# An encoder kernel on one core: layer 0 projects in float32 without splits, u is rearranged by copies, RoPE in six operations, a new order of the work

## The chip, the cores and the metric

The kernel runs on one core of one Trainium2 chip. The metric is the device time of one execution in microseconds. A core has TensorE (PE, matrix products into PSUM), VectorE (DVE), ScalarE (ACT), GpSimd (POOL), and SyncE (SP), which in this kernel only issues DMAs.

## The reference

Two pre-norm layers work on 256 tokens of width 1024 in float32. Each layer has a token mixer and a mixture of experts:

```
xn = rmsnorm(x, ln1_g);  proj = xn @ w_in
qa, ka, va, u, cq, ckv, kr = split(proj)        # 384 128 128 256 192 128 32 columns
o_attn = windowed_gqa(qa, ka, va, sink)         # 6 heads, 2 kv heads, window 128, ALiBi
o_ssm  = s5_bidirectional(u, ...)               # 16 groups x 64 complex states, two directions, GLU
o_mla  = mla(cq, ckv, kr, ...)                  # 6 heads of 64 + 32 rotary, low-rank q and kv
x = x + concat(rmsnorm each of the three) @ w_out
x = x + hier_moe(rmsnorm(x, ln2_g), ...)        # 4 groups x 8 experts, top group, top 2 of it
```

Each expert has a gate, an up (1024 x 256) and a down matrix (256 x 1024). After the two layers comes a last rmsnorm. RoPE turns the 32 rotary columns of q (six heads) and of the one shared key: (x1 cos - x2 sin, x1 sin + x2 cos).

## The kernel before, in words

**Buffers.** All weights stream through a ring of 25 SBUF buffers of 128 x 2048 float32 (1 MB each). SP issues their DMAs in one fixed order: the mixer's weights (u, nat, qk, mla, gr, o), then for each block of experts the gate and up halves and the down matrices, then layer 1. The mixer's temporaries take buffers of the same ring. `make_plan` counts from the written order how many temporaries each step needs, and `room` lets a weight be fetched only if the steps up to its use still have their buffers. When no buffer is free, the stream stands still.

**Order.** `SEQ` is a string for each layer: the mixer's steps in the order in which they are emitted, each with letters that choose the engine of its optional operations (V VectorE, S ScalarE, G GpSimd). The framework then orders each engine's instructions around that. Steps of the mixer: x (transposed input), u, n0 n1 (columns in token order: va, cq, ckv, kr), q0 to q3 (columns transposed: q and k), uc (u by place), t0 to t4, td, i, w, c (tables of the state space layer), s0 s1 (its products with the inputs), S0 S1 (its scans, one direction each), so and gl (its output and GLU), a/A/V (scores, weights, values of the windowed attention), la lq lk lv l0 to l2 lr m/M/W (the same of the latent attention), G (norms of the groups), O (output projection by group, token half, column half), R r e h k (router).

**Splits.** For the letters in `SPLIT` of a layer a float32 product is made of three passes in float32r: `parts` makes a rounded high half on ScalarE and the low half on VectorE or GpSimd (line 672), `halved` does it for the input of layer 0 (line 717), and `mm` (line 682) issues high x high, high x low, low x high. Layer 0 splits n and q, layer 1 u, n and q, and the output projection is split in both; `finish` writes its left side as a high and a low half (line 854). Without a split `mm` issues one float32 product.

**u by place.** `u_chunks` picks every fourth token of u and sets the four picks on top of each other, 32 channels each, with 32 products with slices of the identity (line 748), and one copy out of PSUM.

**RoPE.** `latent_q` makes six operations for each token half, all on the engine that one letter picks (lines 955 to 960).

**Experts.** `moe` gathers each expert's tokens by products with one-hot matrices, four or two experts beside each other in TensorE's columns (line 1441 gate and up, line 1457 down), and adds the results back to x. A block's buffers come free as its products end.

Of the kernel before, what the change touches and what calls it, by code (L numbers as in the profile page):

```python
# [22 lines left out]
T = 256  # L23
# [5 lines left out]
SEQ = ("x:VSGGVSVG t1 x0:V x1:G t2:GVGSSV pn0:GGGG t3 pn1:VGGG x3:V sq x2:V u b0 n0 rb:SVV pq0:GVVV n1:SVVS "  # L29
# [10 lines left out]
SPLIT = ("nq", "unq")  # L40
# [10 lines left out]
        "gl": ("ub", "qkv", "hT", "hTl"), "R": KEEP, "r0": KEEP, "r1": KEEP, "e0": KEEP, "e1": KEEP, "h0": (), "h1": (), "k0": (), "k1": (),  # L51
# [111 lines left out]
def hybrid_encoder_kernel(ctx, tc, I, out, dbg=None):  # L163
# [402 lines left out]
    def uses(l, w):  # L566

        hs = ["hT", "hTl"]
# [6 lines left out]
        if w in USES:  # L575
            u = list(USES[w])
# [7 lines left out]
        elif w[0] == "p":  # L584
            u = wp(w[1], w[1:])
        elif w[0] == "P":
            u = [f"o{w[1]}h", f"o{w[1]}l"]
        elif w[0] in "aA":
            u = ["PB" if w[1] == "2" else "PA"] + (["qkv", "bs"] if w[0] == "a" else ["pt"])
        elif w[0] == "m":  # L590
            u = ["qT", "kT", "PB" if w[1] in "45" else "PM"]
        elif w[0] == "M":
            u = ["PB" if w[1] == "2" else "PM", "pt"]
        elif w[0] in "VW":
            u = ["pt", "ub", "qkv" if w[0] == "V" else "cTvm"] + hs
        elif w[0] == "O":
            u = [f"o{int(w[1]) + i}{p}" for i in range(2) for p in "hl"] + hs
        else:
            u = []
        return u  # L600

    def eats(l, w):
# [9 lines left out]
        if w[0] == "P":  # L612
            return [(l, "o", int(w[1]))]
        return [(l, "gr")] if w in ("gl", "e0", "e1") else []

    def mixer(l):
# [10 lines left out]
        def hs():  # L627
            return [sub(n, 0, (8, T)).bitcast(F32R) for n in ("hT", "hTl")]
# [56 lines left out]
        with tc.tile_pool(name=f"mx{l}", bufs=1, reuse_waits="tile") as mp:  # L685
# [7 lines left out]
            def transposed():  # L693

                xT = xs("u")
                for k in range(8):
# [10 lines left out]
                    pk = p[:, 256 * (k % 2):256 * (k % 2) + 256]  # L707
                    S.activation(xT[0][:, k, :], pk, AF.Copy, scale=g)
# [35 lines left out]
            def u_chunks():  # L744
                u4p = ps("u4p")
                for j in range(4):
                    for i in range(8):
                        PE.matmul(u4p[32 * j:32 * j + 32, 64 * i:64 * i + 64], ident[:, 32 * (i % 4):32 * (i % 4) + 32],
                                  uT()[:, i // 4, :].rearrange("p (q j) -> p j q", j=4)[:, j, :],
                                  start=True, stop=True, tile_position=(0, 32 * j))  # L750
                copy(u4().rearrange("p i q -> p (i q)"), u4p)
# [98 lines left out]
            def finish(c, g, k, vg, src):  # L850
# [3 lines left out]
                V.scalar_tensor_tensor(hT[1][:, k, :], src, gc, hT[0][:, k, :].bitcast(F32), op0=OP.mult, op1=OP.subtract)  # L854
# [84 lines left out]
            def latent_q():  # L939
                mw, q, ra4 = page(l, "mla"), qn(), sub("qn", 1344, (4, 7, 16))  # L940
                G.memset(q[:, :, 6, 0:64], 0.0)
                for tt in range(2):
# [7 lines left out]
                    G.tensor_copy(q[:, tt, 6, 64:96], nat()[:, tt, 320:352])  # L950
                for tt in range(2):
                    x1, x2 = q[:, tt, :, 64:80], q[:, tt, :, 80:96]
                    cb, sb = cos[:, tt].to_broadcast([128, 7, 16]), sin[:, tt].to_broadcast([128, 7, 16])
                    e = pick("VG")
                    e.tensor_tensor(ra4[:, 0], x1, cb, OP.mult)
                    e.tensor_tensor(ra4[:, 1], x2, sb, OP.mult)
                    e.tensor_tensor(ra4[:, 2], x1, sb, OP.mult)
                    e.tensor_tensor(ra4[:, 3], x2, cb, OP.mult)
                    e.tensor_tensor(x1, ra4[:, 0], ra4[:, 1], OP.subtract)
                    e.tensor_tensor(x2, ra4[:, 2], ra4[:, 3], OP.add)  # L960
# [94 lines left out]
            def out_proj(g, tt, hf):  # L1055
                k0, n = ((0, 3), (3, 2), (5, 3))[g]
                p, hT = ps("op"), hs()
                for k in range(k0, k0 + n):
                    mm(p, [t[:, k, 128 * tt:128 * tt + 128] for t in hT],
                       [w[:, k % 2, 512 * hf:512 * hf + 512] for w in win[f"o{k // 2}"]], k == k0, k == k0 + n - 1)  # L1060
# [46 lines left out]
    class Router:  # L1107


        def __init__(self, l):  # L1110
# [16 lines left out]
            self.xk = x.rearrange("p t (d k) -> p t k d", k=8)  # L1127

# [4 lines left out]
        def tokens(self, tt):  # L1133
            S.activation(self.junk, x[:, tt, :], AF.Square, accum_out=self.ssq[:, tt:tt + 1])
# [561 lines left out]
```

## Time and profile before

| what | value |
|---|---|
| median of 3 runs | 772.03 us (771.19 to 775.95) |
| the profiled execution: time, span | 773.82 us, 772.0 us |
| PE busy | 654.1 us, 85% of the span |
| DVE, ACT, POOL busy | 384.6, 256.6, 162.5 us |
| moved by DMA | 232.93 MB, mean 302 GB/s |

The span runs from the first to the last instruction. Busy time of an engine is the time in which at least one of its instructions ran; matrix products are pipelined, so a busy PE is not PE at its peak. The granted clock is the mean clock that TensorE was given in a stretch, as a share of full speed. Layer 0's mixer takes the first 174 us or so, layer 1's about 403 to 525 us; the expert layers follow them.

### The profile page before, as it was taken

What the parts mean: (1) busy time and instruction counts of PE and PEld (TensorE: products, weight loads), DVE (VectorE), ACT (ScalarE), POOL (GpSimd) and SP (SyncE); (2) the same over time, 40 slices, a digit from 0 to 9 for tenths busy, and PEclk for the clock granted to TensorE, in tenths of its full rate; (3) what the DMA queues carried; (4) which work ended last, traced back from release to release, by engine and by line L of the source; (5) the groups of instructions that cost most, each with busy time, mean ns of one, the idle gap of its engine ahead of it and who ended that gap; (6) DMA issues with size and microseconds to landing.
All of it is one profiled execution on the core that took longest, in us unless ns stands there. A gap on an engine that the chain in (4) does not pass through costs nothing. (4 is left out here: it accounts for less than half of the span.)

```text
span 772.0 us, 12384 instructions
## 1 busy us (share of the span) xinstructions
PE 654.1 (85%) x4546; PEld 406.7 (53%) x4546; DVE 384.6 (50%) x872; ACT 256.6 (33%) x574; POOL 162.5 (21%) x180
## 2 busy tenths in 40 slices
PE   7599498998979778669889989998989988859994
PEld 6388386774425425135538967785545334324342
DVE  3978975643233413842436868863343232422324
ACT  2563477432201212442325268614212111011113
POOL 2654634300000001332004254530000000000001
PEclk9799797999989989878999999998999999979998
DMA  8910017489799979999999153599599999997991
GB/s 304 420 68 1 0 46 284 134 315 411 300 410 407 412 246 414 414 410 413 406 405 402 58 175 110 198 356 391 197 416 408 402 409 414 415 378 287 410 366 59
DMA packets 57209, 232.93 MB, mean 302 GB/s; under 512 B 6048, under 2 KB 8480, under 8 KB 48160
## 3 DMA queue, kind: packets, MB, share of 16 engines
q1 hardware_dynamic: 57120, 231.75, 77.5%
q8 instruction: 55, 0.90, 0.5%
q14 instruction: 34, 0.28, 0.1%
HBM read 233.82 MB, written 1.05 MB: 304 GB/s over the span
## 5 line engine op out<-in xcount | busy, mean ns | idle before, releaser
L1441 PE MATMUL gu<-pg,xe 128*32 128x512 f32 (+1 forms) x1024 | 150.1, 624 | 10.0 <-DMA pg<-in_w_up_dram 8.1
L1457 PE MATMUL yp<-pg,scr 128*32 128x512 f32 (+2 forms) x560 | 79.0, 633 | 26.8 <-DVEq L1588 12.7
L1441 PEld LDWEIGHTS gu<-pg,xe 128*32 128x32 f32 (+1 forms) x1024 | 45.1, 118 | 100.7 <-issue 94.3
L1227 POOL TENSOR_TENSOR pgt<-oh,gate 128x256 f32<-128x256 f32 (+1 forms) x13 | 10.2, 783 | 314.0 <-PE slp L373 304.7
L1235 PE MATMUL gp<-oh,xn 128*128 128x128 f32 (+1 forms) x416 | 71.1, 325 | 3.7 <-DVE oh L1220 1.6
L1235 PEld LDWEIGHTS gp<-oh,xn 128*128 128x128 f32 x416 | 61.4, 197 | 17.2 <-issue 12.3
L1457 PEld LDWEIGHTS yp<-pg,scr 128*32 128x32 f32 (+1 forms) x560 | 22.6, 120 | 73.0 <-issue 56.9
L1360 DVE TENSOR_TENSOR y<-yp,y 128x512 fp32r<-128x512 f32 (+1 forms) x39 | 26.2, 676 | 68.3 <-ACT y L1359 68.3
L1252 DVE TENSOR_TENSOR x<-cp,x 128x512 f32<-128x512 f32 x76 | 48.8, 683 | 20.2 <-PE cp L1251 20.2
L1347 DVE SCALAR_TENSOR_TENSOR scr<-gu,gs,scr 128x256 f32<-128x256 f32 x19 | 9.1, 481 | 87.1 <-ACT scr L1346 83.1
L1359 ACT CAST y<-yp 128x512 fp32r<-128x512 f32 (+1 forms) x39 | 22.3, 575 | 88.6 <-PE yp L1457 87.1
L356 ACT ACTIVATE xe<-gp,vec 128x128 f32<-128x128 f32 (+1 forms) x52 | 21.3, 409 | 73.1 <-PE gp L1235 73.1
L360 DVE TENSOR_SCALAR xe<-gp,vec 128x128 f32<-128x128 f32 (+1 forms) x52 | 20.8, 400 | 48.4 <-PE gp L1235 48.3
L1346 ACT ACTIVATE scr<-gu 128x256 f32<-128x256 f32 x19 | 7.3, 384 | 98.3 <-PEq L1558 50.7
L1250 PE MATMUL cp<-y,sm 128*128 128x512 f32 x76 | 33.5, 450 | 0.3 <-PEq L1558 0.2
L1251 PE MATMUL cp<-y,sm 128*128 128x512 f32 x76 | 30.0, 403 | 1.5 <-DVE y L1360 1.5
L1062 DVE SCALAR_TENSOR_TENSOR x<-op,rg,x 128x512 f32<-128x512 f32 x24 | 17.9, 747 | 17.4 <-PE op L682 14.2
L1340 ACT ACTIVATE scr<-slp 128x256 f32<-128x256 f32 x20 | 7.7, 387 | 46.4 <-SPq L1423 27.6
L1250 PEld LDWEIGHTS cp<-y,sm 128*128 128x128 f32 x76 | 14.3, 189 | 10.4 <-issue 8.2
L373 PE MATMUL slp<-cst,pgt 128*128 128x128 f32 x36 | 8.3, 314 | 12.1 <-DVE oh L1220 6.1
L373 PE MATMUL hp<-cst,scr 128*128 128x128 f32 x40 | 9.2, 312 | 10.9 <-DVE scr L1347 9.8
L549 PE MATMUL t4p<-ca,tabs 128*32 128x32 f32 (+3 forms) x512 | 16.3, 250 | 2.0 <-issue 2.0
(460 smaller groups left out, 1353.1 us busy)
## 6 DMA issues: line engine op xcount, KB each, us to landing
pg<-in_w_gate_dram SPq DMA_DIRECT2D x128, 512.0 KB, 10.2
pg<-in_w_up_dram SPq DMA_DIRECT2D x128, 512.0 KB, 10.2
pg<-in_w_down_dram SPq DMA_DIRECT2D x56, 1024.0 KB, 12.1
pg<-in_w_o_dram SPq DMA_DIRECT2D x8, 1024.0 KB, 17.9
pg<-in_w_down_dram SPq DMA_DIRECT2D x12, 512.0 KB, 10.4
pg<-in_w_qk_dram SPq DMA_DIRECT2D x4, 1024.0 KB, 16.3
pg<-in_w_nat_dram SPq DMA_DIRECT2D x4, 960.0 KB, 14.2
wgu<-in_w_gate_dram SPq DMA_DIRECT2D x4, 512.0 KB
```

Of the source, the lines that this page charges most:

```text
L356: S.copy(dst, src) if scale is None else S.activation(dst, src, AF.Copy, scale=scale)
L360: e.tensor_scalar(dst, src, scale, None, op0=OP.mult)
L373: PE.transpose(dst, src, ident[:src.shape[0], :src.shape[0]])
L1062: V.scalar_tensor_tensor(xh, p, rg[:, g, tt:tt + 1], xh, op0=OP.mult, op1=OP.add)
L1235: PE.matmul(p[:, :w], xn[:, tt, k, :], P[:, tt].rearrange("p e c -> p (e c)"), start=(tt == 0), stop=(tt == 1))
L1250: PE.matmul(p, Sm[:, 128 * tt:128 * tt + 128], yh[:, c], start=True, stop=False)
L1251: PE.matmul(p, Sm[:, 128 * tt:128 * tt + 128], yl[:, c], start=False, stop=True)
L1252: V.tensor_tensor(x[:, tt, c], p, x[:, tt, c], OP.add)
L1359: S.copy(yh[:, c], yp)
L1360: V.tensor_tensor(yl[:, c], yp, yh[:, c].bitcast(F32), OP.subtract)
L1441: PE.matmul(gu[m * s:m * s + m, :].rearrange("p (a f) -> p a f", a=2), xs(k, s), page(l, "gu", e, hf)[:, :, k % 4, :], start=(k == 0), sto ...
L1457: PE.matmul(yp[m * s:m * s + m, :], hT[:, j, m * s:m * s + m], page(l, "dn", e)[:, j, c], start=(j == 0), stop=(j == 1), tile_position=(0, ...
```

## The change

Layer 0 no longer splits anything: n, q and the output projection are float32 products on the weights as they arrived, and the input and the left side of the output projection exist once. So the steps pn, pq, P and x0 to x3 leave layer 0's order, `O` eats the weight buffers itself, and the split buffers are not taken. u is rearranged in both layers by 16 copies of 32 partitions (the letters behind uc alternate VectorE and ScalarE). RoPE is four products over both halves and all heads and two sums over both token halves, on VectorE. Layer 0 has a new order and new letters, most of which move work from GpSimd to VectorE or ScalarE. The router takes its two buffers at its first use (`pages`, called by `tokens`) and not at R.

```diff
--- before.py
+++ after.py
@@ -26,18 +26,17 @@
 ORDER = (((24, 2), (0, 4), (4, 4), (26, 2), (8, 4), (12, 4), (16, 4), (20, 4), (28, 4)),
          ((16, 2), (0, 4), (18, 2), (4, 4), (8, 4), (12, 4), (20, 4), (24, 4), (28, 4)))
 UNIT_PREP, UNIT_AT, TAB_AT = (3, 4), (3, 5), 4
-SEQ = ("x:VSGGVSVG t1 x0:V x1:G t2:GVGSSV pn0:GGGG t3 pn1:VGGG x3:V sq x2:V u b0 n0 rb:SVV pq0:GVVV n1:SVVS "
-       "ue i0:VVVSSVVVSS q1 w0:SSSV uc:S q0 b1 i1:GGVVSGGVSS w1:SSSV la:VVVSVSS pq1:VVVG s0 td:G q3 "
-       "S0:VGVVGG s1 a0 S1:GGGGGG b2 lq:SSSSVV a1 lk:SSSSSS q2 A0:VVSSVS l1:S lr c0:GGVVVSSVGVSS l0:V a2 "
-       "c1:VVVSVVVGVV R V0:V l2:V A1:VVVVVV m1 lv:SS t4 P1:GVGG V1:SG m3 m5 A2:GGSGGS P0:VVVV m2 m0 V2:VG so "
-       "M0:SSSSSV m4 G0 gl:VSG M1:SSSSSS W0:S P2:GVGG O000 G1 O010 W1:VV M2:GSVVGS P3:VVVV O110 W2:SV O100 "
-       "O001 G2 O201 O101 O200 O211 r0:VS O011 e0 O210 O111 h0 r1:VV e1 h1 k0 k1:V",
-       "b0 pu:GGGV x sq u rb:VVV ue pn0:GVVV b1 n0 uc:V pq0:GVGV s0 pn1:VVVG S0:VVVVVV q1 s1 pq1:GGVG "
-       "n1:SVSS S1:GGGVVG q0 q3 q2 la:SSSSSSV a0 lk:SVSSVV b2 a1 a2 lq:SSSSVV P0:GGGG so A0:SGSSSS R lv:VV "
-       "l0:S A1:GGVGGV l1:V lr V0:V l2:S A2:VSVVGV m2 V1:SG V2:SG m1 m5 m3 P1:VGGV m4 m0 G0 O000 gl:VVV O011 "
-       "M0:VVSGVS M1:VSSVGV W0:S M2:SVSVVV W1:VV P2:GGGG W2:VG G1 O111 O001 P3:GVGV O010 G2 O201 O101 O200 "
-       "O100 O110 O211 O210 r0:VV r1:VS e0 e1 h1 h0 k0 k1:V")
-SPLIT = ("nq", "unq")
+SEQ = ("x:VSSSSVVV t1 t2:GVVSVV u t3 sq b0 i0:VVVSSVVVSS n0 rb:SVV n1:SSVV ue uc:VVVSVSVSVSVSVSVS q1 w0:SSSV "
+       "i1:VVVVVVVVSV q0 w1:VSSS la:SVSSVSV s0 td:V q3 b1 S0:VVVVVV s1 a0 b2 c0:GGVVVSSVVVSS lq:SSSS lk:SSSSSS a1 q2 "
+       "A0:SVVSVS l1:S lr l2:V lv:SS l0:S S1:VVVVVV m2 c1:VVVSVVVVVV m1 V0:V a2 R A1:SSSVSS t4 A2:VVSSVS m3 m5 m0 m4 "
+       "V1:SV V2:SV so M0:VSVSVV G0 gl:VVV M1:SVSSSS W0:V M2:VSVVVS O000 G1 O010 O110 W2:SV O101 W1:SV O100 O001 O011 "
+       "G2 O201 O200 O211 r0:VV O210 e0 h0 O111 r1:VV e1 h1 k1:V k0",
+       "b0 pu:GGGV x sq u rb:VVV ue pn0:GVVV b1 n0 uc:VSVSVSVSVSVSVSVS pq0:GVGV s0 pn1:VVVG S0:VVVVVV q1 s1 pq1:GGVG "
+       "n1:SVSS S1:GGGVVG q0 q3 q2 la:SSSSSSV a0 lk:SVSSVV b2 a1 a2 lq:SSSS P0:GGGG so A0:SGSSSS R lv:VV l0:S "
+       "A1:GGVGGV l1:V lr V0:V l2:S A2:VSVVGV m2 V1:SG V2:SG m1 m5 m3 P1:VGGV m4 m0 G0 O000 gl:VVV O011 M0:VVSGVS "
+       "M1:VSSVGV W0:S M2:SVSVVV W1:VV P2:GGGG W2:VG G1 O111 O001 P3:GVGV O010 G2 O201 O101 O200 O100 O110 O211 O210 "
+       "r0:VV r1:VS e0 e1 h1 h0 k0 k1:V")
+SPLIT = ("", "unqo")
 TABLES = "t0 | t1 t2 | t3 td i0 | w0 i1 | w1 | c0 c1 | t4 |"
 STATE = ("ws0", "ws1", "rot", "dect4", "ca0", "ca1")
 KEEP = ("xe", "xn")
...
@@ -565,7 +564,7 @@
 
     def uses(l, w):
 
-        hs = ["hT", "hTl"]
+        hs = ["hT", "hTl"] if "o" in SPLIT[l] else ["hT"]
 
         def xs(w):
             return ["xT", "xTl"] if w in SPLIT[l] else ["xR"]
@@ -573,7 +572,7 @@
         def wp(w, n):
             return [n + "h", n + "l"] if w in SPLIT[l] else []
         if w in USES:
-            u = list(USES[w])
+            u = list(USES[w]) + (hs if w == "gl" else [])
         elif w[0] in "nq":
             u = xs(w[0]) + wp(w[0], w if w[0] == "n" else f"q{int(w[1]) // 2}") + (["ub"] if w[0] == "q" else []) + \
                 (["qkv"] if w[0] == "q" or w == "n1" else [])
@@ -594,7 +593,7 @@
         elif w[0] in "VW":
             u = ["pt", "ub", "qkv" if w[0] == "V" else "cTvm"] + hs
         elif w[0] == "O":
-            u = [f"o{int(w[1]) + i}{p}" for i in range(2) for p in "hl"] + hs
+            u = [f"o{int(w[1]) + i}{p}" for i in range(2) for p in "hl" if "o" in SPLIT[l]] + hs
         else:
             u = []
         return u
@@ -611,6 +610,8 @@
             return [(l, "mla")]
         if w[0] == "P":
             return [(l, "o", int(w[1]))]
+        if w[0] == "O" and "o" not in SPLIT[l]:
+            return [(l, "o", int(w[1]) + i) for i in range(2)]
         return [(l, "gr")] if w in ("gl", "e0", "e1") else []
 
     def mixer(l):
@@ -625,7 +626,7 @@
             return [sub(n, 0, (8, T)).bitcast(F32R) for n in ("xT", "xTl")] if w in split else [sub("xR", 0, (8, T))]
 
         def hs():
-            return [sub(n, 0, (8, T)).bitcast(F32R) for n in ("hT", "hTl")]
+            return [sub(n, 0, (8, T)).bitcast(F32R) for n in ("hT", "hTl")] if "o" in split else [sub("hT", 0, (8, T))]
 
         def qaT():
             return sub("qkv", 0, (3, T))
@@ -705,6 +706,9 @@
                                 transpose(p[:, 256 * j + 128 * tt:256 * j + 128 * tt + 128],
                                           x[:, tt, 128 * (k + j):128 * (k + j) + 128])
                     pk = p[:, 256 * (k % 2):256 * (k % 2) + 256]
+                    if "u" not in split:
+                        copy(xT[0][:, k, :], pk, g, "SV")
+                        continue
                     S.activation(xT[0][:, k, :], pk, AF.Copy, scale=g)
                     V.scalar_tensor_tensor(xT[1][:, k, :], pk, g, xT[0][:, k, :].bitcast(F32), op0=OP.mult,
                                            op1=OP.subtract)
@@ -742,13 +746,11 @@
                     V.tensor_tensor(uT()[:, c, :], held["u"][c][:, :T], rb(), OP.mult)
 
             def u_chunks():
-                u4p = ps("u4p")
+
                 for j in range(4):
-                    for i in range(8):
-                        PE.matmul(u4p[32 * j:32 * j + 32, 64 * i:64 * i + 64], ident[:, 32 * (i % 4):32 * (i % 4) + 32],
-                                  uT()[:, i // 4, :].rearrange("p (q j) -> p j q", j=4)[:, j, :],
-                                  start=True, stop=True, tile_position=(0, 32 * j))
-                copy(u4().rearrange("p i q -> p (i q)"), u4p)
+                    for g in range(4):
+                        copy(u4()[32 * j:32 * j + 32].rearrange("p (c g) q -> p c g q", g=4)[:, :, g, :],
+                             uT()[32 * g:32 * g + 32].rearrange("p c (q j) -> p c j q", j=4)[:, :, j, :])
 
 
             def s5_states(d):
@@ -851,7 +853,9 @@
 
                 gc, sq, hT = vc[:, vg + c:vg + c + 1], sub("ub", 1024, (2, T)), hs()
                 copy(hT[0][:, k, :], src, gc, "VS")
-                V.scalar_tensor_tensor(hT[1][:, k, :], src, gc, hT[0][:, k, :].bitcast(F32), op0=OP.mult, op1=OP.subtract)
+                if "o" in split:
+                    V.scalar_tensor_tensor(hT[1][:, k, :], src, gc, hT[0][:, k, :].bitcast(F32), op0=OP.mult,
+                                           op1=OP.subtract)
                 if c == 0:
                     S.activation(sqs[g], src, AF.Square)
                 else:
@@ -937,7 +941,7 @@
                     pin(G.tensor_scalar(tri, iota, cst[:, C_P:C_P + 1], None, op0=OP.is_ge))
 
             def latent_q():
-                mw, q, ra4 = page(l, "mla"), qn(), sub("qn", 1344, (4, 7, 16))
+                mw, q, ra = page(l, "mla"), qn(), sub("qn", 1344, (2, 7, 32))
                 G.memset(q[:, :, 6, 0:64], 0.0)
                 for tt in range(2):
                     for hf in range(2):
@@ -948,16 +952,15 @@
                                   mw[:64, 1344 + 288 * hf:1632 + 288 * hf], start=False, stop=True)
                         copy(q[:, tt, 3 * hf:3 * hf + 3, :].rearrange("p h d -> p (h d)"), p[:, :288])
                     G.tensor_copy(q[:, tt, 6, 64:96], nat()[:, tt, 320:352])
+
                 for tt in range(2):
-                    x1, x2 = q[:, tt, :, 64:80], q[:, tt, :, 80:96]
-                    cb, sb = cos[:, tt].to_broadcast([128, 7, 16]), sin[:, tt].to_broadcast([128, 7, 16])
-                    e = pick("VG")
-                    e.tensor_tensor(ra4[:, 0], x1, cb, OP.mult)
-                    e.tensor_tensor(ra4[:, 1], x2, sb, OP.mult)
-                    e.tensor_tensor(ra4[:, 2], x1, sb, OP.mult)
-                    e.tensor_tensor(ra4[:, 3], x2, cb, OP.mult)
-                    e.tensor_tensor(x1, ra4[:, 0], ra4[:, 1], OP.subtract)
-                    e.tensor_tensor(x2, ra4[:, 2], ra4[:, 3], OP.add)
+                    cb, sb = (t[:, tt].unsqueeze(2).to_broadcast([128, 7, 2, 16]) for t in (cos, sin))
+                    xh = q[:, tt, :, 64:96].rearrange("p h (a c) -> p h a c", a=2)
+                    V.tensor_tensor(ra[:, tt].rearrange("p h (a c) -> p h a c", a=2), xh, sb, OP.mult)
+                    V.tensor_tensor(xh, xh, cb, OP.mult)
+                x1, x2 = q[:, :, :, 64:80], q[:, :, :, 80:96]
+                V.tensor_tensor(x1, x1, ra[:, :, :, 16:32], OP.subtract)
+                V.tensor_tensor(x2, x2, ra[:, :, :, 0:16], OP.add)
 
             def latent_k():
                 mw = page(l, "mla")
@@ -1057,7 +1060,7 @@
                 p, hT = ps("op"), hs()
                 for k in range(k0, k0 + n):
                     mm(p, [t[:, k, 128 * tt:128 * tt + 128] for t in hT],
-                       [w[:, k % 2, 512 * hf:512 * hf + 512] for w in win[f"o{k // 2}"]], k == k0, k == k0 + n - 1)
+                       [w[:, k % 2, 512 * hf:512 * hf + 512] for w in weights(f"o{k // 2}", "o", k // 2)], k == k0, k == k0 + n - 1)
                 xh = x[:, tt, 512 * hf:512 * hf + 512]
                 V.scalar_tensor_tensor(xh, p, rg[:, g, tt:tt + 1], xh, op0=OP.mult, op1=OP.add)
 
@@ -1125,12 +1128,17 @@
             pin(V.tensor_tensor(self.wr, self.wr, self.vc[:, V_LN2:V_LN2 + 8].unsqueeze(2).to_broadcast([128, 8, 40]),
                                 OP.mult))
             self.xk = x.rearrange("p t (d k) -> p t k d", k=8)
+            self.xe = None
+
+        def pages(self):
 
             self.xe = work["xe"]
             self.xT, self.xn = page_sm(self.xe, 0, (8, T)), page_sm(work["xn"], 0, (2, 8, 128))
             self.junk = self.xn[:, 1].rearrange("p k d -> p (k d)")
 
         def tokens(self, tt):
+            if self.xe is None:
+                self.pages()
             S.activation(self.junk, x[:, tt, :], AF.Square, accum_out=self.ssq[:, tt:tt + 1])
             rstd(self.r2[:, tt:tt + 1], self.ssq[:, tt:tt + 1], 1.0 / D)
             for k in range(0, 8, 4):
```

## Rows read from the trace of the kernel before

**Rows 1.** The page: span, and DMA busy share in 40 slices.
```profile
span 772.0 us, 12384 instructions
...
DMA  8910017489799979999999153599599999997991
```

**Rows 2.** Busy time of each engine, granted clock, DMA share, by stretch of the mixers.
```profile
0.00:174.00 174.00, 142.95 (x1083) 118.08 (x1084) 125.56 (x276) 88.16 (x186) 72.86 (x83) 0.90 0.47 175
16.00:50.00 34.00, 21.18 (x89) 16.27 (x89) 32.16 (x69) 18.41 (x34) 20.77 (x16) 0.80 0.77 317
50.00:84.00 34.00, 34.00 (x267) 29.68 (x265) 28.48 (x52) 16.56 (x41) 13.70 (x20) 1.00 0.00 1
84.00:100.00 16.00, 4.94 (x28) 4.25 (x26) 12.58 (x34) 7.29 (x19) 9.90 (x9) 0.68 0.00 1
100.00:140.00 40.00, 36.76 (x466) 30.13 (x465) 28.11 (x73) 28.64 (x72) 15.12 (x15) 0.87 0.51 186
140.00:175.00 35.00, 32.88 (x184) 26.22 (x183) 21.40 (x52) 13.90 (x20) 7.80 (x12) 1.00 0.67 234
403.00:525.00 122.00, 116.31 (x791) 96.26 (x790) 90.74 (x200) 65.03 (x147) 55.85 (x60) 0.99 0.61 227
```

**Rows 3.** TensorE's waits, 16 to 175 us: total, times, longest.
```profile
PE ptp L373 <- DVE PA L360: 11.1, 1, 11.1
```

**Rows 4.** Timeline of TensorE: start, duration, operation, count.
```profile
10.52 5.51 PE L682 MATMUL up<-xR,pg 128*128 128x256 f32 x24 [0.55 <-POOL xR L360]
...
30.34 0.37 PE L682 MATMUL natp<-n0h,xT 128*128 128x480 f32 x1
30.55 0.38 PE L682 MATMUL natp<-n0l,xT 128*128 128x480 f32 x1
...
50.63 6.18 PE L748 MATMUL u4p<-ub,cst 128*32 128x64 f32 x64
...
57.55 0.28 PE L682 MATMUL qkp<-xT,q0h 128*128 128x256 f32 x1
57.67 0.28 PE L682 MATMUL qkp<-xTl,q0h 128*128 128x256 f32 x1
...
73.46 0.75 PE L945 MATMUL qn<-pg,cTvm 128*128 128x288 f32 x2
74.14 0.75 PE L947 MATMUL qn<-pg,cTvm 64*128 64x288 f32 x2
...
139.95 0.40 PE L682 MATMUL op<-o0h,hT 128*128 128x512 f32 x1
140.18 0.39 PE L682 MATMUL op<-o0l,hT 128*128 128x512 f32 x1
...
668.57 7.03 PE L1410 MATMUL guu<-wgu,xu 128*128 128x512 f32 x16
```

**Rows 5.** Busy time of line 672 (low halves) on VectorE and GpSimd, layer 0.
```profile
0.00:174.00 174.00, 17.20 (x17) 21.51 (x15) 0.90 0.47 175
```

**Rows 6.** Timeline of VectorE.
```profile
29.30 0.68 DVE L486 SCALAR_TENSOR_TENSOR w<-w 128x512 f32<-128x512 f32 x1
30.01 0.29 DVE L358 COPY tabs<-tabs 64x256 f32<-64x256 f32 x1
...
90.24 1.32 DVE L955 TENSOR_TENSOR qn<-qn,cst 128x112 f32<-128x112 f32 x1
91.48 0.26 DVE L956 TENSOR_TENSOR qn<-qn,cst 128x112 f32<-128x112 f32 x1
```

**Rows 7.** A group of ScalarE copies in layer 0: count, busy, mean ns.
```profile
L356 ACT COPY kT<-knp 64x256 f32<-64x256 f32 x6 | 2.2, 365 | 0.1
```

**Rows 8.** Timeline of GpSimd, 88 to 92 us.
```profile
88.91 2.52 POOL L792 TENSOR_TENSOR zz<-cd 128x504 f32<-128x504 f32 x2
```

**Rows 9.** Waits of SP's DMA queue, 20 to 204 us: total, times, longest.
```profile
SPq L248 <- PE t4p L549: 70.7, 1, 70.7
...
SPq L248 <- PE yp L1457: 6.7, 1, 6.7
```

More of the change, by code (lines that the diff above doesn't have):

```diff
@@ L50 @@
         "l2": ("qn", "qT"), "lr": ("qn", "kT"), "so": ("dect4", "ca0", "ca1", "zz", "ub", "qkv"),
-        "gl": ("ub", "qkv", "hT", "hTl"), "R": KEEP, "r0": KEEP, "r1": KEEP, "e0": KEEP, "e1": KEEP, "h0": (), "h1": (), "k0": (), "k1": (),
+        "gl": ("ub", "qkv"), "R": (), "r0": KEEP, "r1": KEEP, "e0": KEEP, "e1": KEEP, "h0": (), "h1": (), "k0": (), "k1": (),
         "b0": ("bs",), "b1": ("bs",), "b2": ("bs",), "G0": (), "G1": (), "G2": ()}
```

## The prediction

> **What bounds the kernel now.** I read the page first, then a table of stretches, the waits of TensorE and of SP's queue, and last single instructions. On the page the DMA line has two holes, slices 3 to 6 and 23 to 26 (19.3 us each), and is near full elsewhere [rows 1]. The holes are the mixers of the two layers; the full parts are the expert layers, which the weight stream paces. So a microsecond counts where the stream stands still because the ring's buffers are full.
>
> The table [rows 2] gives the mixer of layer 0 by stretch. From 16 to 50 us DVE is busy 32.2 of 34 us while PE has 21.2 us of work at a mean granted clock of 0.80: PE waits for halves of weights. From 50 to 84 PE is full at 1.00. From 84 to 100 it has 4.9 us of work; one transpose alone waits 11.1 us for DVE [rows 3]. From 140 to 175 PE is full again. Layer 1's mixer, 403 to 525, is the yardstick: PE busy 116 of 122 us at 0.99, with DVE at 91.
>
> **The change, part by part.**
>
> *Float32 projections in layer 0: PE.* A split product is three passes: 0.217 us apart at 480 columns, 0.12 at 256, 0.23 at 512 [rows 4]. So n is 16 x 3 x 0.217 = 10.4, q 32 x 3 x 0.12 = 11.5, the output projection 32 x 3 x 0.23 = 22.1: 44 us. A float32 product shows as two records. The u projection takes 5.51 us for 24, 0.46 per product of 256 columns; full-array products of 512 columns take 7.03 us for 16, 0.88 each [rows 4]. For 480 columns I scale the latter: 0.82. So n costs 13.1, q 14.7, o 28.2: 56 us, 12 more. The unfavourable bound is the row where 288 columns take 0.68 (73.46 to 74.14 us, weight rows alternating 128 and 64) [rows 4]; by columns that is 77 us, 33 more. The favourable one is 512-column pace throughout: 11 more. I take 12, because u is the same helper and weight shape.
>
> *Splits gone.* The low halves cost DVE 17.2 and POOL 21.5 us in layer 0 [rows 5], besides ACT's casts. None of that is work for the new form. What it is worth on PE follows by stretch below.
>
> *u by place.* 64 records in 6.18 us [rows 4] leave PE in each layer, with one evacuation. In their place stand 16 copies of 32 partitions x 128 elements, nine on DVE and seven on ACT in layer 0, eight and eight in layer 1. Such a copy is not in the trace. Bounds: 0.29 (DVE, 64x256) or 0.365 (ACT, 64x256) above [rows 6, 7], half of that below. Nine at 0.26, as a product of 112 elements takes alone [rows 6], in parallel with ACT make 2.3 us, so the chain to the state products gets some 4.5 us shorter and PE 6.2 us emptier. Behind the copies DVE has the low halves of n1 in layer 1, which PE needs last in its next step.
>
> *RoPE.* Twelve operations become six of twice the elements. One of 112 elements takes 0.26 alone and 1.32 beside POOL's products [rows 6, 8]; five of layer 0's twelve fell so, about 5 x 1.32 + 7 x 0.26 = 8.4 us. Six at 0.4 take 2.4, at most 8 if each waits. I take 2.4 in layer 0, since POOL loses its products there.
>
> *New order and engines, layer 0.* Fifteen 128x512 products go from POOL to DVE (four in i1, nine in the two scans, two in c0 and c1). At 0.68 [rows 6] that is 10 us more on DVE, but a pair such as POOL's 2.52 us [rows 8] becomes 1.4, in the chain.
>
> *Router buffers later.* xe and xn are taken at r0 and not at R, and 16 split buffers vanish. By the plan's own rule, counted through the written orders, 13 buffers of expert weights are asked for by the step "so" instead of 6, but 22 by the last output projection in both. SP now waits 70.7 us for a buffer in the mixer, and later 6.7 us for the last products of the first expert block [rows 9]: there the ring is full already. So earlier prefetch adds nothing behind that point; the expert layer moves by what the mixer gains, one for one. I cost it at nothing.
>
> **The sum, by stretch of layer 0** [rows 2]. 16 to 50: about 15 us of full-speed PE work (n 10.4, one q group 2.9, small transposes) stand in 34; the new form has 18.5 and no split to wait for; with 2.5 us lost to arrivals, -13 (bounds -4, if the state tables on DVE hold the next stage, to -16). 50 to 84: -6.2 for u, +2.5 for three q groups, -3.7 (0 to -6). 84 to 100: RoPE and the POOL tail of the scan fill it; -7 (0 to -11). 100 to 140: the o splits go, and the clock of 0.87 says that PE waited; -4 (0 to -10). 140 to 175: +6, all of it on PE (+5 to +17). Together -22. As a check: PE is busy 129.8 us from 16 to 175, about 117 at full speed by the stretches' clocks; 12 more and 6.2 less make 123; at layer 1's 95% density that ends near 146, a gain of 28. I stay at 22 because layer 0 carries the state tables besides.
>
> Layer 1: the 6.2 us of PE and the evacuation go where PE is dense, 2 us of copies come: -5 (bounds -7 to +3). RoPE there hides under PE work, and if that cover went it would cost 2 us.
>
> Total -27. The profiled execution took 773.8 us (span 772.0 and 1.8 around it), 1.8 above the median of 772.0. So 746.8 against its own time, 745 against the median.
>
> **The rivals.**
>
> *DVE becomes the bound of layer 0.* For: DVE is the busy engine from 16 to 84 [rows 2], and 10 us of products plus 2.3 of copies come to it. Against: about 17 of splits and 6 of RoPE go [rows 5, 6]. If the scans and state tables are strung on DVE, the first three stretches give -11 rather than -24, the fourth nothing, the last costs 6: -5, and -5 in layer 1: 762.
>
> *The copies wait for POOL in layer 1.* POOL still splits q and n there when they run. Beside a POOL operation the small product took 1.06 us longer [rows 6, 8]; eight copies so delayed make 8.5 us, and layer 1 turns from -5 to +3: 753. The Trainium skill, "SBUF — State Buffer", section "Who interferes with whom", says that a float32 copy on VectorE in its two-port mode and a GpSimd operation shut each other out for a whole instruction. The rows show it for a product with two inputs; none shows it for a copy.
>
> *The stream holds the end of layer 0.* The DMA line is full to the end of the expert layer [rows 1]; if the stream and not the first block set it, only layer 1 gives: 767. Against it stand SP's 6.7 us at full buffers [rows 9].
>
> *Denser than layer 1.* If PE never waits: -32 and -6: 734.
>
> *Slower: float32 at the lower clock.* A granted clock of 0.68 and 0.80 in two stretches [rows 2] means part of them at 1.2 GHz. If the 56 us of projections ran at that level they would take 112, and 27 gained becomes 29 lost: 801. It turns the sign once about half of them run so (27 of 56). Against: both low stretches had gaps in PE's work before them, and the full ones have 1.00.
>
> **How the numbers follow.** Forecast 0.55, around 745 (736 to 754); copies waiting 0.10; DVE-bound 0.17; stream 0.07; denser 0.06; slower 0.05. The range 734 to 763 takes in the forecast with its bounds, the copies, the denser case and most of DVE-bound. 1% is 7.7 us, about what this kernel's runs can tell. Faster by more: 0.55 + 0.10 + 0.06 + 0.15 of DVE-bound = 0.86; within 1%: the rest of that and the stream, 0.09; slower 0.05.
>
> **What would show it.** Right: n products with two records 0.41 us apart at a clock of 1.00 from about 16 us; no split before layer 1; no PE gap of 11 us; the first gate product some 22 us sooner; SP still waiting for a product of the first expert block; in layer 1 the state products straight behind n0, about 6 us sooner. Wrong: DVE over 95% busy through a stretch in which PE waits; copies of 1 us or more; a mixer of layer 0 shorter by 20 with an expert layer longer by as much.

## The result: 750.6 us, 3.2% faster, and the profile after

The changed kernel took 750.62 us (median) beside 773.99 of the kernel before: ratio 0.968, 95% interval 0.962 to 0.975. One of its four executions, 759.4 us, counts as slow, and the ratio leaves it out. The forecast was 745 in 734 to 763. The profiled execution took 747.92 us, its span is 746.1, 25.9 shorter than that of [rows 1].

The page after, first line, engines, granted clock and DMA share in 40 slices:

```profile
span 746.1 us, 11906 instructions
...
PE 640.8 (86%) x4338; PEld 376.8 (51%) x4338; DVE 361.8 (48%) x875; ACT 245.0 (33%) x570; POOL 107.1 (14%) x135
...
PEclk9999999999899899789999999979999998969998
DMA  8920798384999799999994616994999999979971
```

The first hole of the DMA line is two slices wide where [rows 1] has four. By stretch (columns as in [rows 2]):

```profile
16.00:46.00 30.00, 27.56 (x129) 19.03 (x129) 28.61 (x78) 18.78 (x44) 5.59 (x7) 1.00 0.86 353
46.00:61.00 15.00, 15.00 (x85) 11.06 (x84) 15.00 (x34) 4.21 (x8) 4.34 (x9) 1.00 0.01 1
61.00:76.00 15.00, 10.89 (x52) 8.39 (x51) 14.48 (x39) 13.33 (x37) 0.23 (x2) 0.89 0.15 49
76.00:90.00 14.00, 12.52 (x280) 10.27 (x279) 10.09 (x36) 8.71 (x28) 0.00 (x0) 1.00 0.92 324
90.00:120.00 30.00, 28.02 (x221) 20.37 (x220) 15.83 (x41) 13.97 (x38) 1.80 (x4) 1.00 0.87 320
120.00:150.00 30.00, 28.46 (x113) 15.52 (x112) 12.46 (x30) 7.31 (x10) 2.37 (x6) 1.00 0.50 184
378.00:493.00 115.00, 108.58 (x712) 88.81 (x710) 89.51 (x196) 65.52 (x151) 53.54 (x59) 0.98 0.66 239
```

TensorE, which had 21.2 of 34 us of work at 0.80 in the first of these stages [rows 2], is busy 27.6 of 30 at 1.00. VectorE is now full from 46 to 76 (29.5 of 30 us). The stretch with 4.9 of 16 us of TensorE work is gone; its one long wait [rows 3] is 4.1 us, on another engine (TensorE's waits, 16 to 150 us):

```profile
PE ptp L372 <- ACT PA L355: 4.1, 1, 4.1
PE t4p L548 <- issue: 2.3, 1, 2.3
PE natp L683 <- DMA pg<-in_w_nat_dram: 1.7, 1, 1.7
```

The float32 products on TensorE's timeline (first of each kind, with the count of the run), and the first gate product of layer 0's experts:

```profile
17.37 3.08 PE L683 MATMUL natp<-pg,xR 128*128 128x480 f32 x7 [1.71 <-DMA pg<-in_w_nat_dram]
...
31.01 3.62 PE L683 MATMUL qkp<-xR,pg 128*128 128x256 f32 x16
...
123.04 7.13 PE L683 MATMUL op<-pg,hT 128*128 128x512 f32 x16
...
154.53 1.97 PE L1449 MATMUL gu<-pg,xe 128*64 128x512 f32 x4
```

The whole group of n takes 13.15 us for 32 records, q 3.62 for 16, o 7.13 for 16: 0.82, 0.45 and 0.89 us per product of two records. SP still waits for a product of the first expert block (its queue's waits, 100 to 180 us; 6.7 in [rows 9]):

```profile
SPq L247 <- PE yp L1465: 10.0, 1, 10.0
```

### The profile page after: what moved, and what is told of

Read it like the earlier page. It is cut to its first block, busy times and chain, and to the rows that moved or that the text cites. A ratio compares the mean times of both kernels' runs of the same rounds, so it can differ in the third digit from the quotient of the medians.

```text
span 746.1 us, 11906 instructions
## 1 busy us (share of the span) xinstructions
PE 640.8 (86%) x4338; PEld 376.8 (51%) x4338; DVE 361.8 (48%) x875; ACT 245.0 (33%) x570; POOL 107.1 (14%) x135
## 3 DMA queue, kind: packets, MB, share of 16 engines
HBM read 233.82 MB, written 1.05 MB: 315 GB/s over the span
## 5 line engine op out<-in xcount | busy, mean ns | idle before, releaser
L1449 PE MATMUL gu<-pg,xe 128*32 128x512 f32 (+1 forms) x1024 | 152.7, 636 | 10.7 <-DMA pg<-in_w_up_dram 9.6
L1243 PEld LDWEIGHTS gp<-oh,xn 128*128 128x128 f32 x416 | 61.9, 198 | 18.1 <-issue 10.9
L355 ACT ACTIVATE xe<-gp,vec 128x128 f32<-128x128 f32 (+1 forms) x52 | 21.2, 409 | 69.1 <-PE gp L1243 68.1
L683 PE MATMUL op<-pg,hT 128*128 128x512 f32 x64 | 29.1, 599 | 0.0
L372 PE MATMUL slp<-cst,pgt 128*128 128x128 f32 x36 | 8.3, 314 | 17.2 <-issue 11.4
L1258 PEld LDWEIGHTS cp<-y,sm 128*128 128x128 f32 x76 | 14.3, 189 | 10.7 <-issue 8.6
## 6 DMA issues: line engine op xcount, KB each, us to landing
pg<-in_w_gate_dram SPq DMA_DIRECT2D x128, 512.0 KB, 10.1
pg<-in_w_down_dram SPq DMA_DIRECT2D x12, 512.0 KB, 10.7
```

The lines of the kernel that those rows point to most:

```text
L355: S.copy(dst, src) if scale is None else S.activation(dst, src, AF.Copy, scale=scale)
L683: PE.matmul(p, lhs[i], rhs[j], start=start and n == 0, stop=stop and n == len(pairs) - 1)
L1243: PE.matmul(p[:, :w], xn[:, tt, k, :], P[:, tt].rearrange("p e c -> p (e c)"), start=(tt == 0), stop=(tt == 1))
L1258: PE.matmul(p, Sm[:, 128 * tt:128 * tt + 128], yh[:, c], start=True, stop=False)
L1449: PE.matmul(gu[m * s:m * s + m, :].rearrange("p (a f) -> p a f", a=2), xs(k, s), page(l, "gu", e, hf)[:, :, k % 4, :], start=(k == 0), sto ...
```

## Where the 25.9 us came from

I cut each profiled execution at the same instructions: the last router product of layer 0, the first u product of layer 1, the last router product of layer 1, the last product of all. The last column is TensorE's wait at its first instruction behind layer 1's overflow expert. "Time" is a median of timed runs, the ratio is to runs of the kernel before on the same chip; the other columns come from one execution each. Between kernels that have the same code in a stage they differ: by 3.7 us in mixer 0 (changed and e5), by 4.1 in mixer 1 (changed and e10), by up to 4 in expert layer 0, and by 6.6 in expert layer 1 with the same wait (e8 and e11). A smaller difference between two kernels in one column can be chance.

```
kernel                      time   ratio (95% interval)    mixer 0  experts 0  mixer 1  experts 1  wait
before                      774.0                          172.3    232.7      115.3    242.5       6.1
changed                     750.6  0.968 (0.962 to 0.975)  149.0    228.6      110.7    248.6      11.4
e1  copies alone            778.6  1.005 (1.001 to 1.010)  179.0    232.5      112.0    245.2       6.1
e2  RoPE alone              773.3  1.000 (0.997 to 1.004)  170.9    234.6      114.2    244.7       5.9
e3  float32 alone           759.5  0.983 (0.978 to 0.988)  158.9    229.9      116.4    242.1       6.1
e4  all, old order+engines  757.2  0.979 (0.976 to 0.983)  162.6    231.4      111.3    241.9       5.9
e8  all, old order          746.9  0.966 (0.962 to 0.970)  154.4    229.4      111.1    241.4       6.1
e6  changed, old engines    758.8  0.984 (0.980 to 0.988)  158.3    229.4      111.4    247.5      11.3
e9  changed, u4p in layer 0 753.0  0.975 (0.971 to 0.979)  156.0    229.7      111.5    245.4       6.0
e5  changed, u4p in layer 1 752.5  0.975 (0.970 to 0.979)  152.7    229.9      114.8    242.7       6.0
e7  changed, buffers at R   748.3  0.969 (0.964 to 0.974)  148.5    230.1      110.1    248.3      11.6
e12 changed, RoPE in twelve 752.6  0.972 (0.967 to 0.976)  149.0    232.4      113.2    248.3      11.6
e10 changed, six more       747.1  0.965 (0.961 to 0.969)  149.8    231.3      114.8    242.5       6.1
e11 e8, six fewer           754.1  0.974 (0.970 to 0.979)  155.5    229.4      111.0    248.0       6.1
```

Of the 25.9 us the mixer of layer 0 gave 23.3, that of layer 1 4.6, the first expert layer 4.0; the second took 6.1 back.

## The experiments

**e1, e2, e3: each part alone.** In e1 the 32 products (64 records) of `u_chunks` give way to the 16 copies in both layers; in e2 `latent_q` is the new one; in e3 `SPLIT = ("", "unqo")`, the steps x0 to x3, pn, pq and P of layer 0 are gone, the router's buffers are taken late as in the changed kernel, and all else is old. The edit of e1 in the order strings, cut to the step `uc`:

```diff
-"... uc:S q0 b1 ..."                 (layer 0)      -"... uc:V pq0:GVGV ..."  (layer 1)
+"... uc:VVVSVSVSVSVSVSVS q0 b1 ..."                 +"... uc:VSVSVSVSVSVSVSVS pq0:GVGV ..."
```

> The kernel before with one part of the change: u by place made by sixteen copies in both layers, all else as before. My theory (the parts add; u4p leaves PE and the chain to the state products gets shorter): 4.5 us off in layer 0 and 5 in layer 1, 764 to 765 against 774. Rival (DVE is the bound of layer 0's mixer): nine more copies on a DVE that is busy 32 of 34 us earn nothing there, only layer 1 gives, 769. Rival (copies wait for POOL, which still splits q and n in layer 1): copies of 1 us and more in the trace, 774 to 778. In the trace a copy should take 0.2 to 0.4 us.

Measured: 0.5% slower (778.6, four executions from 773.0 to 780.2; the profiled one is the slowest). Layer 1's mixer came 3.3 us shorter, layer 0's 6.7 longer in that execution, which no theory had. The copies are not slow: nine in 2.52 us on VectorE. What stands behind them is late. ScalarE, GpSimd and TensorE of e1 in layer 0:

```profile
52.62 2.57 ACT L347 COPY ub<-ub 32x128 f32<-32x128 f32 x6
...
56.16 1.90 ACT L347 COPY gg<-w 64x512 f32<-64x512 f32 x3
```
```profile
61.28 0.52 POOL L332 TENSOR_SCALAR rr<-sq 128x2 f32<-128x2 f32 x1 [2.08 <-ACT ub L909]
```
```profile
56.83 3.60 PE L364 MATMUL wsp<-cst,gg 128*128 128x128 f32 x16 [2.39 <-ACT gg L347]
...
65.55 3.51 PE L747 MATMUL sr<-ub,ws 128*128 128x64 f32 x16
```

The same of the kernel before:

```profile
51.75 1.89 ACT L356 COPY gg<-w 64x512 f32<-64x512 f32 x3
...
58.81 0.19 POOL L341 TENSOR_SCALAR rr<-sq 128x2 f32<-128x2 f32 x1 [3.44 <-ACT ub L920]
...
62.11 1.90 PE L758 MATMUL sr<-ub,ws 128*128 128x64 f32 x16
```

ScalarE's state-table copies (gg) start 4.4 us later, the norm on GpSimd 2.5, the state products 3.4; TensorE, with the 6.2 us of u4p gone, waits, and then does the same 16 state products at the lower clock, in 3.51 us instead of 1.90. In the old order u4p [rows 4] filled time in which TensorE waited for tables anyway; the copies went to the two engines that make them. The late start is only part of the loss: the first score product of the windowed attention starts at 81.05 in e1 and at 72.39 before, 8.7 us later and not 3.4. TensorE had idled, and then ran 11 us at half of its full clock (columns as in [rows 2]):

```profile
55.00:65.00 10.00, 4.41 (x20) 3.81 (x21) 6.39 (x13) 6.40 (x16) 4.52 (x7) 0.76 0.00 0
65.00:76.00 11.00, 11.00 (x54) 10.96 (x52) 6.11 (x9) 2.71 (x4) 2.11 (x4) 0.50 0.01 1
```

> The kernel before with RoPE in six operations on DVE in both layers, all else as before. My theory: RoPE stands in the part of layer 0 where PE is 4.9 of 16 us busy and the chain runs over DVE, so most of the 6 us is seen: 768 to 770 against 774. Rival (RoPE is hidden behind the scan's products on POOL, which end the chain there): 773 to 775.

Measured: no change (0.997 to 1.004), 1.4 us in layer 0's mixer, within its spread. The rival's time is met, but its reason is not shown, because the six operations were not the 2.4 us of the forecast. Beside GpSimd's products five of them took 1.1 to 1.5 us, and together they took 6.9 (8.5 for the twelve before). Two of e2's, and GpSimd beside the second:

```profile
86.09 1.45 DVE L946 TENSOR_TENSOR qn<-qn,cst 128x224 f32<-128x224 f32 x1
90.18 1.44 DVE L950 TENSOR_TENSOR qn<-qn 128x224 f32<-128x224 f32 x1
```
```profile
88.62 2.75 POOL L783 TENSOR_TENSOR zz<-cd 128x504 f32<-128x504 f32 x2
```

How much of a faster RoPE would have been hidden, e2 cannot tell.

> The kernel before with layer 0's projections in float32 without splits, u by place by products and RoPE in twelve as before, steps in the old order on the old engines (POOL keeps its products of the state tables and scans). My theory, from the stretches: -13 from 16 to 50, +2.5 for three q groups, -4 from 100 to 140, +6 from 140 to 175: 8 to 9 us off, 765. Rival (the splits were hidden and the chain of state tables and scans on DVE and POOL holds the mixer): PE's 12 us more decide, 774 to 786. In both, n products of 0.82, q of 0.46, o of 0.88 us.

Measured: some 14 us off, 13.4 of it in layer 0's mixer. Faster than my 8 to 9; the rival is out.

**e4, e8, e6: engines and order.** e4 is the changed kernel with layer 0's old order and letters, e8 with the old order and the new letters, e6 with the new order and the old letters in five steps, shown here side by side (e8 differs from e4 in more letters than these):

```diff
-i1:VVVVVVVVSV S0:VVVVVV S1:VVVVVV c0:GGVVVSSVVVSS c1:VVVSVVVVVV
+i1:GGVVSGGVSS S0:VGVVGG S1:GGGGGG c0:GGVVVSSVGVSS c1:VVVSVVVGVV
```

> The changed kernel, all three parts, but layer 0's steps in the order of before and on its engines (fifteen products stay on POOL). My theory (order and engines are worth the 1.1 us per pair of products that move from POOL to DVE, some 5 us): 754 to 758 where the changed kernel has 750. Rival (the new order carries the gain: in the old one POOL's scan still ends the chain at 100 us): 765 or more. If this kernel has 750 or less, order and engines are worth nothing.

> All three parts of the change and the new engines, but layer 0's steps in the order of before. Theory A (the engines carry the 13.6 us): 744 to 751. Theory B (the order carries it): 756 to 758. If both this run and the one with the old engines lie between, the two act together.

> The changed kernel in its new order, but with the fifteen products of layer 0's state tables and scans (i1, the two scans, c0 and c1) on POOL as before. Theory A (the engines carry what the order run lost, 13.6 us in the mixer of layer 0): first gate product of layer 0 some 10 us later, 758 to 761. Theory B (the order of the steps carries it): 750 to 752. My prediction's price, 1.1 us per pair: 3 to 5 us, 754 to 755.

Measured: e4 757.2, e8 746.9, e6 758.8. From e3 to e4, which adds copies and RoPE, layer 0's mixer is 3.7 us longer, although its state products start sooner, at 47.42 instead of 50.08. From there TensorE runs at the lower clock, as in e1 (first row e4, second row e3 from its first state product):

```profile
47.40:57.50 10.10, 10.10 (x43) 9.38 (x42) 7.03 (x12) 1.71 (x4) 1.06 (x3) 0.51 0.01 2
```
```profile
50.08:60.18 10.10, 10.10 (x78) 9.69 (x77) 8.30 (x12) 0.93 (x2) 1.26 (x1) 1.00 0.00 0
```

Two of e4's copies also ran beside GpSimd's 512-column products, which no copy of the changed kernel does. They took 1.05 and 1.06 us where the others took 0.25 to 0.27:

```profile
35.95 1.05 DVE L349 COPY ub<-ub 32x128 f32<-32x128 f32 x1
```
```profile
35.73 2.21 POOL L496 TENSOR_TENSOR w<-tabs,sp 128x512 f32<-128x512 f32 x2
```

From e4 the engines bring layer 0's mixer 8.2 us (162.6 to 154.4), some 5 of them because that stretch is gone (at half the clock its 10.1 us hold 5 us of work); the order brings 5.4 more (to 149.0). Put the other way round, old engines in the new order cost 9.3. Theory A holds for most of it, and the price of some 5 was too small. The wait [rows 3] explains e6, 10.7 us beside 4.1 in the changed kernel, and in part e8, 8.0; it does not measure the engines in the old order, for it is 6.8 in e4.

```profile
PE ptp L364 <- ACT PA L347: 10.7, 1, 10.7
```
```profile
PE ptp L364 <- ACT PA L347: 8.0, 2, 7.2
```

The second fence is e8's. Yet e8 is no slower than the changed kernel: its second expert layer is 7.2 us shorter (below).

**e9, e5: the copies, undone in one layer each.** `if l == 0:` (e9) or `if l:` (e5) puts the old body back.

> The changed kernel with u by place made by products again in layer 0 alone (copies stay in layer 1). Theory A (from the run with copies alone: in layer 0 the u products ran while TensorE would have waited for the state tables on VectorE and ScalarE, and the copies lengthen those two): the mixer of layer 0 gets 3 to 6 us shorter, 744 to 748 against 750. Theory B (my prediction's pricing: with the new order TensorE is dense, 25.9 of 30 us from 46 to 76, so 6.2 us of products cost some 4 to 6): 754 to 757.

Measured: layer 0's mixer 7.0 us longer; theory A falls, and the sign of e1 does not carry over to the new order and engines. TensorE of e9, and what VectorE waits for behind it:

```profile
33.07 6.24 PE L745 MATMUL u4p<-ub,cst 128*32 128x64 f32 x64 [2.40 <-DVE ub L738]
...
50.40 1.90 PE L761 MATMUL sr<-ub,ws 128*128 128x64 f32 x16
```
```profile
43.00 0.42 DVE L816 TENSOR_TENSOR qkv<-qkp,ub 128x256 f32<-128x256 f32 x1 [3.73 <-PE qkp L675]
```

Here TensorE is the late engine: behind u4p stand the q products and table transposes for which VectorE waits 3.7 us. In the changed kernel the copies stand there and the state products start at 43.55, 6.9 us sooner:

```profile
34.36 2.50 DVE L357 COPY ub<-ub 32x128 f32<-32x128 f32 x9
...
34.89 3.01 ACT L355 COPY ub<-ub 32x128 f32<-32x128 f32 x7
...
43.55 1.90 PE L760 MATMUL sr<-ub,ws 128*128 128x64 f32 x16
```

> The changed kernel with u by place made by products again in layer 1 alone. My prediction's price of -5 in layer 1: last router product of layer 1 some 4 to 5 us later after the first u product of that layer (115 us after it where the changed kernel has 111), 754 to 756. Rival (the 6 us that layer 1's expert layer gave back are given back because the mixer came out shorter): mixer 4 longer, expert layer 4 to 6 shorter, 750. Whether TensorE's wait behind the overflow expert of layer 1 is 6.1 us, as before the change and in four other variants, or 11.4 as in the changed kernel, tells whether that wait hangs on this part.

Measured: 752.5, mixer of layer 1 4.1 us longer (forecast 4 to 5), experts 5.8 shorter. One pair of executions would not show the 4.1, but the table does: the four kernels with products in layer 1 have 114.2 to 116.4, nine with copies 110.1 to 113.2, and the tenth, e10, 114.8 at a lower clock (below). The rival's sum looks met, but not its reason: the wait fell from 11.4 to 6.0, and e9, whose mixer of layer 1 kept its gain, shows the same wait. Layer 0's mixer is 3.7 longer in e5 although nothing was edited there; its granted clock is 0.88 from 16 to 30 us, where the changed kernel has 1.00.

**e10, e11: the 6 us given back.** TensorE at that place, changed kernel and e10:

```profile
652.32 0.74 PE L1259 MATMUL cp<-y,sm 128*128 128x512 f32 x2 [0.40 <-DVE y L1368]
664.49 0.66 PE L372 MATMUL slp<-cst,pgt 128*128 128x128 f32 x2 [11.43 <-issue]
```
```profile
659.89 0.74 PE L1259 MATMUL cp<-y,sm 128*128 128x512 f32 x2 [0.40 <-DVE y L1368]
666.74 0.66 PE L372 MATMUL slp<-cst,pgt 128*128 128x128 f32 x2 [6.11 <-DVE oh L1228]
```

The overflow expert runs under a condition; one runs, and all engines then jump over the code of six more. In the DMA view of the gap code arrives as packets of its own (queue, packets, MB): changed kernel from 653 to 664.5, then e10 from 660.6 to 667:

```profile
q8 instruction: 2, 0.03, 1.2%
q14 instruction: 4, 0.03, 0.7%
```
```profile
q8 instruction: 1, 0.02, 1.1%
q14 instruction: 3, 0.02, 0.9%
```

```diff
-    for i in range(14):
+    for i in range(20):
         PE.matmul(warm[:, :128], ones, ones, start=True, stop=True)
```

> The changed kernel with six more of the warm-up products that TensorE runs before its first weights (twenty instead of fourteen): all later TensorE code lies six instructions further on. Theory C (TensorE's wait of 11.4 us behind the overflow expert of layer 1 is the loading of its own code after a jump, and hangs on where the jump's target lies in a block of code: by a count of the program it stood at place 86 or 87 of 128 in the two kernels that waited 11.3 to 11.4, and elsewhere, 92 among them, in the eight that waited 6): the wait falls to 6 us, the end comes 5 us sooner, 744 to 746. Rival (the wait hangs on the step order or on what the transfers do at that moment): it stays at 11.4 and the time at 750 to 751.

Measured: the wait is 6.1 and the second expert layer 242.5 (248.6). All four kernels with the new order and this number of TensorE products waited 11.3 to 11.6; the three of that order with 6 or 32 products more waited 6.0 to 6.1. The traces of all fourteen kernels agree on what ends the wait: in the ten short ones a single packet of queue 8 (16 KB) lands in it, 3.8 to 4.0 us after its start, in the four long ones a second, 9.5 to 9.8 us after it, and TensorE goes on some 2 us behind the last. So within this order it hangs on where TensorE's code lies, in that the gap takes one block of code more; whose code the packet holds the view does not tell. The Trainium skill, "Runtime: NRT & Kernel Launch", section "Instruction fetch mechanics", says that a taken branch to code outside the blocks at hand waits for a fetch; the trace agrees, and 6 us is the shorter wait here. The time alone cannot show e10's gain: 745.0 to 751.7 in six runs, median 747.1, and its interval overlaps the changed kernel's. In its profiled execution mixer 1, where nothing was edited, lost 4 us, most of them in ten microseconds at 0.68 (second row, changed kernel at the same work: 1.00). Why the clock fell there is not known: TensorE had been busy 12.7 of the 13 us ahead of it, at 1.00.

```profile
394.00:404.00 10.00, 9.56 (x56) 9.31 (x56) 8.81 (x15) 3.22 (x6) 1.35 (x1) 0.68 0.55 227
```
```profile
390.60:400.60 10.00, 9.59 (x82) 9.29 (x81) 8.79 (x15) 3.25 (x6) 1.36 (x1) 1.00 0.71 288
```

> The reverse test: all three parts and the new engines in the old order, which waited 6.06 us there and took 746.9, with six warm-up products fewer (eight instead of fourteen), so that the jump's target comes to the place it has in the changed kernel. Theory C: the wait rises to 11.3 or 11.4, the time to 751 to 753. Rival: the wait stays at 6, 747.

Measured: a miss. The wait stayed at 6.1, though the time rose to 754.1. TensorE is busy 214.9 us in its second expert layer (e8: 209.5), at a clock of 0.83 instead of 0.91 in the forty microseconds around 628, and idle 33.1 instead of 31.9. So my count of places does not carry from one order to another; why e11 is slower by 7 us than e8 stays open, and with it how much of the second expert layer's 6.1 us the longer wait alone explains: e11 has 248.0 there without it.

**e7, e12: two prices.** e7 has `"R": KEEP` and takes the router's buffers in the constructor; e12 has the old `latent_q` with `lq:SSSSVV`.

> The changed kernel with the router's two buffers taken at the step R again. My prediction's price of taking them later: nothing, 750 to 751, because the ring is full at the first expert block either way. Rival (the two buffers let the stream run ahead in the mixers and the expert layer's 4 us more than the mixer's gain come from that): first gate product of layer 0 as in the changed kernel, but the expert layer of layer 0 some 4 us longer, 754.

Measured: 748.3, and no stage moves by over 1.5 us. Priced right, at nothing.

> The changed kernel with RoPE in twelve operations again, all on VectorE, everything else as changed. Theory A (from 31 to 76 us VectorE is the bound of layer 0: busy 44.3 of 45 us): twelve at 0.26 to 0.3 instead of six at 0.38, some 1 us more on VectorE, 751 to 752. My prediction's price of 6 us: 756. Rival (hidden): 750 to 751. The jump's target lies at the same place as in the changed kernel, so the wait of 11.4 us should stay.

Measured: layer 0's mixer unchanged (148.95 against 148.99), layer 1's 2.5 longer, of which TensorE's work is 1.6 and its waits 0.9; 752.6. The profiled execution (754.2) also has 3.7 more in the first expert layer; all of this lies within the spread of the columns. With no product on GpSimd beside them the twelve follow one another every 0.19 us, so the six save little. The first two of e12:

```profile
60.50 0.27 DVE L951 TENSOR_TENSOR qn<-qn,cst 128x112 f32<-128x112 f32 x1
60.69 0.27 DVE L952 TENSOR_TENSOR qn<-qn,cst 128x112 f32<-128x112 f32 x1
```

## Why the prediction was right, and where only its sum was

- **Float32 on TensorE**: 0.82, 0.45 and 0.89 us per product against 0.82, 0.46 and 0.88. The scaling from u and from the 512-column row holds; the row with 288 columns was rightly left as a bound. The rival at the lower clock is out: every projection of layer 0 ran at 1.00, also the last q group (63.3 to 67.0 us), though the stretch around it has 0.89.
- **By stretch**: the forecast has -13 by 50 us, -16.7 by 84, -23.7 by 100, -27.7 by 140, -22 at the end. The same instructions stand apart by: first table transpose 48.79 to 34.47, -14.3; end of the last q product 84.20 to 66.98, -17.2; first transpose behind the wait of [rows 3] 95.25 to 71.09, -24.2; first output product 139.15 to 111.69, -27.5; last router product, -23.3; first gate product 177.88 to 154.53, -23.4.
- **By part the prices failed**, and that the total still came out is in part luck: the stretches had mostly been read from TensorE's missing work, and there the errors cancelled. RoPE was given 6 us in layer 0: e2 shows 1.4, e12 none. What slowed the small operations was GpSimd beside them, in e2 still, so that gain belonged to the step "new order and engines", which was priced at 1.1 us a pair (e4's expectation: some 5 in all) and measured 8 to 9 for the engines and 5 for the order. The copies in layer 0 were given 4.5 off the chain to the state products as if that did not depend on the rest. These products start 3.4 us later with copies in e1, 2.7 sooner in e4 and 6.9 sooner in the changed kernel than in e9; the mixer changed by +6.7, +3.7 (with RoPE) and -7.0, the two losses with about 10 us of TensorE at half its full clock.
- **The sums**: the check of the total counts 117 us of full-speed work from 16 to 175 us; the stretches' clocks give 119, so it gains about 27 and not 28. The bound by columns is 76 us, not 77. Neither moves the forecast.
- **Layer 1**: -5 forecast, 4.6 measured (e5: 4.1); its state products come 13.5 us after the first u product instead of 20.6. The copies took 0.28 us on VectorE, at the upper bound of 0.29, and 0.43 on ScalarE, above the 0.365. The rival of copies waiting for GpSimd fell because its condition did not hold: GpSimd was idle from 388.6 to 394 when layer 1's ran. Layer 0's ran beside GpSimd's operations of two columns, at 0.28 each. Its price was about right where copies did meet 512-column products: e4's two took 0.8 us longer each, 1.06 forecast.
- **DVE as the bound**: half seen. A sign named as wrong came up: VectorE is busy 14.5 of 15 us, over 95%, from 61 to 76 while TensorE has 10.9 of 15. But the splits and RoPE that left outweigh what came, as the argument against it said; e6 shows that the products are still better there than on GpSimd.
- **"The expert layer moves one for one"** is the step that failed: it put both expert layers at nothing, and they measured -4.0 in the first and +6.1 in the second. These partly cancel, so the sum does not show it. In the second one wait grew by 5.3 us, TensorE's behind the jump; the rest is within what that layer varies. The first is not settled: the kernels with float32 in layer 0 show 228.6 to 232.4, those without 232.5 to 234.6.

## What to carry to other kernels

Here the price of a stretch read from the bound engine's missing work came out, and the sum of the parts did not: an operation moved between engines was worth its time only where the engine that it left was the late one, and the same move changed sign (+6.7, -7.0) with the order around it. When a stage loses more than the late start explains, look at the granted clock behind the gap. Before rating a wide against a narrow operation, look at what ran beside the slow one. A difference of 5 us far from the edit can be the placing of code behind a jump, or only the spread of a stage from one execution to the next: compare the kernels stage by stage, and shift the code by a few instructions before explaining it.

## What the runs showed of the hardware that was not expected

- After a jump over the code of six overflow experts (36 TensorE products each in the kernel's text) TensorE stood 5.9 to 6.1 us in ten executions and 11.3 to 11.6 in four; six products more ahead of it moved it from the longer to the shorter, with one packet fewer of the larger kind in the gap.
- Two executions of the same work with TensorE busy 9.6 of 10 us ran at a granted clock of 0.68 (e10) and of 1.00 (changed); by the clock alone that is about 3 us (9.6 x 0.32).
- Sixteen state products took 1.90 us at a granted clock of 1.00 (before) and 3.51 at 0.50 (e1), where TensorE had been busy 4.4 of the 10 us ahead of them.
- A copy of 32x128 float32 on VectorE took 0.25 to 0.28 us alone or beside GpSimd's two-column operations, and 1.05 us beside GpSimd's product of 512 columns with two inputs (e4).
